# The first four pairs of the feed-forward input: evacuated by ScalarE, multiplied on GpSimd

## The chip, the cores and the metric

One core of one Trainium2 chip runs the whole program. The metric is the device time of one execution in microseconds (us), as the median of several runs. A profile is one further execution, recorded by the hardware profiler. PE is TensorE (its weight loads are PEld), DVE is VectorE, ACT is ScalarE, POOL is GpSimd, SP issues the DMAs of the weights.

## The reference, cut to what matters

A two-layer decoder block on 16 meta tokens and 256 tokens, model width 1024, in float32. Each layer mixes tokens in three branches (retention, a gated linear recurrence, differential attention), and then runs a feed-forward part with a short convolution over time. The change touches only the latter:

```python
def _rms(x):
    xf = x.astype(F32)
    return xf * lax.rsqrt(jnp.mean(xf * xf, axis=-1, keepdims=True) + EPS)

def conv_ffn(hn, w_ffn_in, conv_w, conv_b, w_ffn_out, valid):
    l = hn.shape[1]
    u = jnp.where(valid[None, :, None], hn @ w_ffn_in, 0.0)
    up = jnp.pad(u, ((0, 0), (CONV_W - 1, 0), (0, 0)))
    c = conv_b + sum(conv_w[j] * up[:, j:j + l] for j in range(CONV_W))
    gate, val = jnp.split(c, 2, axis=-1)
    return (jax.nn.silu(gate) * val) @ w_ffn_out

    # per layer
    h = h + mixer(rms_norm(h, norm_mix_g[li]), ...)
    h = h + conv_ffn(rms_norm(h, norm_ffn_g[li]), ...)
```

`w_ffn_in` is 1024 x 5632 (gate and value halves of 2816), `w_ffn_out` 2816 x 1024.

## The kernel before, in words

**Layout.** Activations lie features on partitions, tokens along the free axis: 272 columns in layer 0. In the last layer most projections leave out the first 14 columns, so 258 are computed. Every product of float32 precision is three passes of TensorE over split operands: high part by high part, low part by high part, high part by low part (L900 to L902).

**Weights.** They come as a stream of chunks of eight 128 x 128 tiles in the order of use. For each chunk SP loads `wraw`, ACT rounds it to `whi` (a Copy), and DVE forms the rest `wlo = wraw - whi`. There are 3 buffers of `wraw` and 4 each of `whi` and `wlo`. A chunk feeds 24 matmuls.

**Pairs.** A pair is two output blocks of 128 features that share a PSUM tile `main`, of which there are two. Pair n + 2 writes the tile of pair n, so its first matmul waits until the last reader of pair n is done. A pair of the feed-forward input (name `fi`, 22 in each layer) is 16 weight tiles, thus two chunks and 48 matmuls.

**The norm.** TensorE does not wait for the norm's factor `rstd`. The first four pairs behind a norm multiply by `h` times the gain, and the product gets `rstd` when it leaves PSUM (`evacuate`, which here is a DVE tensor_tensor from `main` into `two_a`). Meanwhile POOL forms `y = h * rstd` in eight instructions, ACT and DVE split each `y` into `xh` and `xl`, and from the fifth pair on the operands are these folded ones (`norm.folded`); then nothing is left to multiply.

**Behind a pair** comes the convolution: ACT writes `two_b` (bias and newest tap, one instruction for each half), DVE adds the two older taps (four SCALAR_TENSOR_TENSOR), ACT applies Silu, DVE multiplies the halves, ACT and DVE split the result into `ghi` and `glo`. For the first four pairs these read `two_a` in SBUF, from the fifth on they read `main` in PSUM. There are two buffers each of `two_a` and `two_b`.

**Order.** No engine's order is written by hand. `_Plan` records all operations with a cost, and `order()` (L448) lists them by a simulated time: on each engine the ready operation with the smallest key goes next. `_Engine.call` (L568) holds the costs. So a changed cost or another operation moves instructions on all engines, and what was once listed is issued in exactly that order, engine by engine, with semaphores between.

**Names with numbers.** The plan numbers its tiles. In layer 0 `main_900`, `main_911`, `main_920` and `main_929` are the first four pairs of the feed-forward input (with `two_a_909`, `_918`, `_927`, `_936` and `two_b_910`, `_919`, `_928`, `_937`), `main_940`, `main_950` and `main_958` the fifth to seventh (`two_b_949`, `two_b_957`, `two_b_965`). In layer 1 the first four are `main_1962`, `_1973`, `_1982`, `_1991` (`two_a_1971`, `_1980`, `_1989`, `_1998`), and the fifth to eighth `main_2002`, `_2012`, `_2020`, `_2028` (`two_b_2011`, `_2019`, `_2027`, `_2035`).

## Time and profile before

| | |
|---|---|
| median of 3 runs (lowest to highest) | 1308.76 us (1308.33 to 1309.17) |
| profiled execution, its own time | 1309.57 us |
| its span, first to last instruction | 1307.8 us |
| granted TensorE clock | 0.999 |
| PE busy | 1295.4 us (99%) |
| DVE busy | 959.0 us (73%) |
| ACT busy | 801.6 us (61%) |
| POOL busy | 169.8 us (13%) |

How to read it: an engine that is busy for 99% of the span sets the time unless its neighbours make it wait, so what matters is where the few microseconds lie in which PE stands still, and who released it. The busy shares of the other engines are averages over stages: in one stage DVE can have no idle time though its share over the whole span is 73%. In the rows of the timeline the columns are start, duration, engine, line, operation, output and inputs, count of merged instructions and, in brackets, idle time before them with the releaser. Instructions of one engine overlap a little (the next one starts before the last one's end is recorded), so the time that one costs its engine is the distance from its start to the next one's.

### The profile page before, as it was taken

To read this page: it belongs to the slowest core of one execution; us is meant where nothing else is said; L and a number is where in the kernel's file an instruction comes from. 1 tells how busy PE (TensorE), PEld (TensorE's weight loads), DVE (VectorE), ACT (ScalarE), POOL (GpSimd) and SP (SyncE) were. 2 spreads that over 40 slices of the span, in tenths; PEclk is the share of its full clock that TensorE was granted. 3 is DMA by queue.
4 is the path that set the end of the run, shared out by engine and by line. 5 is a ranking of instruction groups with operands and counts; after the bars stand their busy time and mean duration, and the time that the engine had idled before them with its cause. 6 is when DMAs were issued, how large, how long until landed. Compare 5 with 4: busy or idle time off the path is not lost.

```text
span 1307.8 us, 28691 instructions
## 1 busy us (share of the span) xinstructions
PE 1295.4 (99%) x11774; PEld 1266.6 (97%) x11774; DVE 959.0 (73%) x1589; ACT 801.6 (61%) x1332; POOL 169.8 (13%) x204
## 2 busy tenths in 40 slices
PE   9999999999999999999999999999999999999998
PEld 8999999999999999999999999999999999999986
DVE  7675787697576789886575757876986867888853
ACT  6747454746676577666456574547565775767643
POOL 5001101312222020000030011012131210200000
PEclk9999999999999999999999999999999999999999
DMA  7644543443544545555555445444445446466553
GB/s 268 202 143 160 168 160 134 146 146 129 193 131 162 179 160 176 182 175 181 177 177 186 162 152 177 150 144 146 156 147 176 142 165 202 144 199 205 200 188 112
DMA packets 60755, 219.06 MB, mean 168 GB/s; under 512 B 6864, under 2 KB 6992, under 8 KB 60624
## 3 DMA queue, kind: packets, MB, share of 16 engines
q1 hardware_dynamic: 60336, 216.71, 49.0%
q8 instruction: 92, 1.51, 0.5%
q10 hardware_dynamic: 288, 0.52, 0.1%
q14 instruction: 39, 0.32, 0.1%
HBM read 216.16 MB, written 1.05 MB: 166 GB/s over the span
## 4 chain that ended last, share of the span: by engine, by line
PE 92%; DVE 5%; ACT 1%; DMA 1%; issue 1%; SPq 0%; POOL 0%; DVEq 0%; ACTq 0%
PE main L900 27%; PE main L902 26%; PE main L901 26%; PE fo L1403 2%; PE fo L1404 2%; PE fo L1405 2%; DVE wlo L592 1%; PE lev L1084 1%; DVE two_b L592 1%; PE ds L1268 1%; PE ro L592 1%; PE ho L592 1%; PE vt L592 1%; DVE two_a L592 1%; PE do L592 1%
## 5 line engine op out<-in xcount | busy, mean ns | idle before, releaser
L900 PE MATMUL main<-xh,whi 128*128 128x272 f32 (+1 forms) x2368 | 689.7, 291 | 0.4 <-ACT whi L592 0.4
L901 PE MATMUL main<-xl,whi 128*128 128x272 f32 (+1 forms) x2368 | 672.9, 284 | 2.0 <-DVE xl L592 2.0
L902 PE MATMUL main<-xh,wlo 128*128 128x272 f32 (+1 forms) x2368 | 673.5, 284 | 1.2 <-DVE wlo L592 1.0
L592 DVE TENSOR_TENSOR wlo<-wraw,whi 128x1024 fp32r<-128x1024 f32 (+1 forms) x411 | 503.4, 1230 | 186.9 <-ACT whi L592 185.9
L592 ACT ACTIVATE whi<-wraw 128x1024 fp32r<-128x1024 f32 (+1 forms) x411 | 427.0, 1042 | 227.7 <-PE main L901 153.4
L901 PEld LDWEIGHTS main<-xl,whi 128*128 128x128 f32 x2368 | 446.1, 188 | 3.0 <-DVE xl L592 2.4
L902 PEld LDWEIGHTS main<-xh,wlo 128*128 128x128 f32 x2368 | 445.8, 188 | 2.8 <-DVE wlo L592 2.7
L900 PEld LDWEIGHTS main<-xh,whi 128*128 128x128 f32 x2368 | 446.2, 188 | 2.1 <-ACT whi L592 0.6
L592 POOL PARTITION_ALL_REDUCE hr<-hsq x36 | 72.0, 2016 | 120.9 <-ACT hsq L592 120.9
L592 DVE SCALAR_TENSOR_TENSOR two_b<-main,small,two_b 128x256 f32<-128x256 f32 (+2 forms) x144 | 65.3, 487 | 26.8 <-ACT two_b L592 25.1
L592 POOL TENSOR_TENSOR y<-h,rstd 128x272 f32<-128x272 f32 x32 | 34.6, 1113 | 317.1 <-ACT rstd L592 317.1
L592 ACT ACTIVATE two_b<-main,small 128x272 f32<-128x272 f32 (+1 forms) x72 | 37.2, 566 | 24.6 <-PE main L902 24.6
L900 PE MATMUL main<-ghi,whi 128*128 128x272 f32 x176 | 51.0, 290 | 0.0
L901 PE MATMUL main<-glo,whi 128*128 128x272 f32 x176 | 50.6, 287 | 0.0
L902 PE MATMUL main<-ghi,wlo 128*128 128x272 f32 x176 | 50.3, 286 | 0.0
L592 POOL COPY tails<-vsrc 128x32 f32<-128x32 f32 x32 | 11.8, 383 | 224.6 <-ACT vsrc L592 224.6
L900 PE MATMUL main<-b0hi,whi 128*128 128x272 f32 (+1 forms) x128 | 38.2, 298 | 0.0
L900 PE MATMUL main<-b1hi,whi 128*128 128x272 f32 (+1 forms) x128 | 37.8, 295 | 0.0
L592 ACT ACTIVATE vsrc<-main 128x544 f32<-128x544 f32 x24 | 15.0, 626 | 35.2 <-PE main L902 35.1
L900 PE MATMUL main<-yhi,whi 128*128 128x272 f32 (+1 forms) x128 | 36.4, 284 | 0.0
L901 PE MATMUL main<-b0lo,whi 128*128 128x272 f32 (+1 forms) x128 | 36.4, 284 | 0.0
L902 PE MATMUL main<-yhi,wlo 128*128 128x272 f32 (+1 forms) x128 | 36.4, 284 | 0.0
(236 smaller groups left out, 1942.3 us busy)
## 6 DMA issues: line engine op xcount, KB each, us to landing
wraw<-in_w SPq DMA_DIRECT2D x402, 512.0 KB, 3.3
h<-in_h SPq DMA_DIRECT2D x4, 272.0 KB, 5.9
dec<-in_dec SPq DMA_DIRECT2D x2, 544.0 KB, 4.9
wraw<-in_w SPq DMA_DIRECT2D x4, 256.0 KB, 5.6
const<-in_const SPq DMA_DIRECT2D x1, 937.0 KB, 6.5
gain<-in_gl SPq DMA_DIRECT2D x1, 512.0 KB, 5.1
out<-y ACTq DMA_DIRECT2D x2, 256.0 KB, 3.0
out<-y SPq DMA_DIRECT2D x2, 256.0 KB, 2.7
```

Source lines behind the costliest of these rows:

```text
L592: self.plan.add(self.name, lambda: f(*args, **kw), cost, outs, ins, args[2] if method == "activation" else None)
L900: nc.tensor.matmul(o, wh, hi, start=first, stop=False)
L901: nc.tensor.matmul(o, wh, lo, start=False, stop=False)
L902: nc.tensor.matmul(o, wl, hi, start=False, stop=last)
L1084: nc.tensor.matmul(o, keys, x, start=True, stop=True)
L1268: nc.tensor.matmul(ss[m][:, at : at + nk], q[half, hd, q0 : q0 + P], k[half, hd, :nk], start=True, stop=True)
L1403: nc.tensor.matmul(o, gh, wh, start=False, stop=False)
L1404: nc.tensor.matmul(o, gl, wh, start=False, stop=False)
L1405: nc.tensor.matmul(o, gh, wl, start=False, stop=end)
```

## The change

`evacuate` gets a flag `aside`, and the feed-forward input passes it. For the first four pairs of that stage, in both layers, the DVE tensor_tensor from PSUM becomes an ACT Copy from `main` to `two_a`, and a POOL tensor_tensor that multiplies `two_a` by `rstd` in place (its key is 2.0 later). That is eight instructions less on DVE, eight more on ACT, eight more on POOL. The plan's costs of POOL change too: a tensor_tensor of n columns goes from 0.04 + 2.45e-3 n to 0.25 + 3.2e-3 n, and a tensor_copy from the same to 0.33 + 0.85e-3 n; the other POOL costs stay.

```diff
             if self.name == "act":
                 cost += 0.093 * (len(aps) - 2) - (0.043 if ins[0].tensor.name in self.plan.psum else 0.0)
-            elif self.name == "pool" and method != "memset":
-                cost += 1.6e-3 * n
+            elif self.name == "pool" and method == "tensor_tensor":
+                cost = 0.25 + 3.2e-3 * n
+            elif self.name == "pool" and method == "tensor_copy":
+                cost = 0.33 + 0.85e-3 * n
...
-    def evacuate(out, ps):
+    def evacuate(out, ps, aside=False):
         factor = pair(rstd[:, T - ps.shape[2] :])
         if norm.folded:
             act.activation(out, ps, AF.Copy)
-        elif norm.adds is pool and norm.pairs == 1:
+        elif aside or norm.adds is pool and norm.pairs == 1:
 
             act.activation(out, ps, AF.Copy)
             plan.key += 2.0
...
-                    evacuate(u, ps)
+                    evacuate(u, ps, True)
```

The branch with ACT and POOL is not new: the very first pair of the program already takes it (`hq`).

The change moves instructions on four of five engines, since the plan is made anew; SP's order stays. Three places matter below. A line of the changed file from the cost rule on has a number higher by two (L594 for L592).

The first place is POOL in layer 0, behind the norm of the feed-forward input. Before, with the copies of the attention's outputs (`da`) ahead of it and the next norm's products behind it:

```order
L592 COPY da_688<-tw_738 128x4x16 x2
L592 ISA
L592 TENSOR_TENSOR y_938<-h_78,rstd_93 128x272 x4
L592 TENSOR_TENSOR y_939<-h_78,rstd_93 128x272 x4
L592 TENSOR_TENSOR y_1202<-h_78,rstd_93 128x272 x4
```

Now:

```order
L594 TENSOR_TENSOR y_938<-h_78,rstd_93 128x272
L594 TENSOR_TENSOR two_a_909<-two_a_909,rstd_93 128x544
L594 TENSOR_TENSOR y_938<-h_78,rstd_93 128x272 x3
L594 TENSOR_TENSOR y_939<-h_78,rstd_93 128x272 x3
L594 TENSOR_TENSOR two_a_918<-two_a_918,rstd_93 128x544
L594 TENSOR_TENSOR y_939<-h_78,rstd_93 128x272
L594 TENSOR_TENSOR two_a_927<-two_a_927,rstd_93 128x544
L594 TENSOR_TENSOR two_a_936<-two_a_936,rstd_93 128x544
```

Four products of 544 columns stand between and behind the eight `y`. In layer 1 the first product (`two_a_1971`) stands ahead of all `y`, the other three behind them.

The second place is DVE in layer 0, around the older taps of the fifth pair (`two_b_949`), the last readers of `main_940`, on which the seventh pair waits. Before:

```order
L592 TENSOR_TENSOR wlo_953<-wraw_951,whi_952 128x1024
L592 SCALAR_TENSOR_TENSOR two_b_937<-two_a_936,small_76,two_b_937 128x271 x2
L592 SCALAR_TENSOR_TENSOR two_b_937<-two_a_936,small_76,two_b_937 128x270 x2
L592 TENSOR_TENSOR wlo_956<-wraw_954,whi_955 128x1024
L592 TENSOR_TENSOR two_b_937<-two_b_937 128x272
L592 SCALAR_TENSOR_TENSOR two_b_949<-main_940,small_76,two_b_949 128x271 x2
L592 SCALAR_TENSOR_TENSOR two_b_949<-main_940,small_76,two_b_949 128x270 x2
L592 TENSOR_TENSOR glo_908<-two_b_937,ghi_907 128x272
L592 TENSOR_TENSOR wlo_961<-wraw_959,whi_960 128x1024
L592 TENSOR_TENSOR two_b_949<-two_b_949 128x272
L592 TENSOR_TENSOR wlo_964<-wraw_962,whi_963 128x1024
```

Now:

```order
L594 TENSOR_TENSOR wlo_956<-wraw_954,whi_955 128x1024
L594 TENSOR_TENSOR two_b_928<-two_b_928 128x272
L594 TENSOR_TENSOR wlo_961<-wraw_959,whi_960 128x1024
L594 TENSOR_TENSOR glo_908<-two_b_928,ghi_907 128x272
L594 SCALAR_TENSOR_TENSOR two_b_937<-two_a_936,small_76,two_b_937 128x271 x2
L594 SCALAR_TENSOR_TENSOR two_b_937<-two_a_936,small_76,two_b_937 128x270 x2
L594 TENSOR_TENSOR wlo_964<-wraw_962,whi_963 128x1024
L594 TENSOR_TENSOR two_b_937<-two_b_937 128x272
L594 SCALAR_TENSOR_TENSOR two_b_949<-main_940,small_76,two_b_949 128x271 x2
L594 SCALAR_TENSOR_TENSOR two_b_949<-main_940,small_76,two_b_949 128x270 x2
L594 TENSOR_TENSOR glo_908<-two_b_937,ghi_907 128x272
```

The weights' rests `wlo_961` and `wlo_964`, both of the seventh pair, stood behind the fifth pair's taps and now stand ahead of them.

The third place is DVE in layer 1, around the older taps of the sixth pair (`two_b_2019`), the last readers of `main_2012`, on which the eighth pair waits. Before:

```order
L592 TENSOR_TENSOR wlo_2026<-wraw_2024,whi_2025 128x1024
L592 TENSOR_TENSOR wlo_2031<-wraw_2029,whi_2030 128x1024
L592 TENSOR_TENSOR glo_2010<-two_b_2011,ghi_2009 128x256
L592 SCALAR_TENSOR_TENSOR two_b_2019<-main_2012,small_76,two_b_2019 128x256 x4
L592 TENSOR_TENSOR wlo_2034<-wraw_2032,whi_2033 128x1024
```

Now:

```order
L594 SCALAR_TENSOR_TENSOR two_b_1999<-two_a_1998,small_76,two_b_1999 128x256 x4
L594 TENSOR_TENSOR two_b_2011<-two_b_2011 128x256
L594 TENSOR_TENSOR wlo_2031<-wraw_2029,whi_2030 128x1024
L594 TENSOR_TENSOR two_b_1999<-two_b_1999 128x256
L594 TENSOR_TENSOR wlo_2034<-wraw_2032,whi_2033 128x1024
L594 TENSOR_TENSOR glo_1970<-two_b_1999,ghi_1969 128x256
L594 TENSOR_TENSOR glo_2010<-two_b_2011,ghi_2009 128x256
L594 TENSOR_TENSOR wlo_2039<-wraw_2037,whi_2038 128x1024
L594 SCALAR_TENSOR_TENSOR two_b_2019<-main_2012,small_76,two_b_2019 128x256 x4
```

Here `wlo_2034` and `wlo_2039` have moved ahead of the sixth pair's taps. Elsewhere, at the start of the program, the two weight chunks of the sixth pair (`wlo_153`, `wlo_156`) and the cast of the masks now stand ahead of the last `xl` piece of the first norm, and PE takes 15 matmuls of the sixth pair ahead of the fifth pair's last six; in layer 1 the softmax steps of the differential attention change places with one another.

## The prediction

> **What bounds the kernel now.** I read the page's first part first, then who PE waited for, then the stretches where those waits lie, then the rows of DVE and POOL there.

> ```profile
> span 1307.8 us, 28691 instructions
> PE 1295.4 (99%) x11774; PEld 1266.6 (97%) x11774; DVE 959.0 (73%) x1589; ACT 801.6 (61%) x1332; POOL 169.8 (13%) x204
> PE main L901 <- DVE xl L592: 2.0, 2, 1.7
> PE main L902 <- DVE wlo L592: 1.0, 4, 0.3
> 490.00:500.00 10.00, 9.64 (x78) 9.41 (x76) 10.00 (x20) 7.60 (x14) 0.00 (x0) 1.00 0.31 108
> 500.00:510.00 10.00, 9.62 (x76) 9.20 (x75) 9.93 (x20) 6.97 (x13) 0.00 (x0) 1.00 0.51 165
> 1130.00:1140.00 10.00, 9.78 (x84) 9.58 (x82) 9.93 (x20) 8.32 (x17) 1.47 (x1) 1.00 0.32 106
> 1140.00:1150.00 10.00, 8.44 (x70) 8.24 (x70) 10.00 (x20) 6.62 (x12) 0.00 (x0) 1.00 0.49 158
> ```

> PE is busy for 99%, so the whole kernel has some 12 us to gain. The columns of the stretches are length, PE, PEld, DVE, ACT, POOL, clock, DMA share and GB/s: around 500 us (layer 0) and 1140 us (layer 1), where the first pairs of the feed-forward input run, PE has holes while DVE has no idle time at all. There DVE is the bound, though its share of the span is 73%. The two largest holes are one late `xl` each:

> ```profile
> 496.19 0.28 PE L900 MATMUL main<-xh,whi 128*128 128x272 f32 x1
> 496.83 0.40 PE L901 MATMUL main<-xl,whi 128*128 128x272 f32 x1 [0.36 <-DVE xl L592]
> 1139.51 0.28 PE L900 MATMUL main<-xh,whi 128*128 128x258 f32 x1
> 1141.44 0.39 PE L901 MATMUL main<-xl,whi 128*128 128x258 f32 x1 [1.66 <-DVE xl L592]
> ```

> Matmuls start 0.12 us apart otherwise, so these cost 0.52 and 1.81 us; the smaller ones on `wlo` behind them some 0.7. About 3.0 us is all that the change could win here. Everything else turns on what DVE loses or gains in these two places, and DVE works beside POOL there:

> ```profile
> 473.31 1.22 DVE L592 TENSOR_TENSOR wlo<-wraw,whi 128x1024 fp32r<-128x1024 f32 x1
> 476.27 0.72 DVE L592 TENSOR_TENSOR two_a<-main,rstd 128x544 f32<-128x544 f32 x1 [1.74 <-ACT rstd L592]
> 476.33 8.47 POOL L592 TENSOR_TENSOR y<-h,rstd 128x272 f32<-128x272 f32 x8 [64.49 <-ACT rstd L592]
> 477.23 1.70 DVE L592 TENSOR_TENSOR wlo<-wraw,whi 128x1024 fp32r<-128x1024 f32 x1 [0.23 <-ACT whi L592]
> 479.60 1.77 DVE L592 TENSOR_TENSOR wlo<-wraw,whi 128x1024 fp32r<-128x1024 f32 x1 [0.67 <-ACT whi L592]
> 481.29 3.80 DVE L592 SCALAR_TENSOR_TENSOR two_b<-two_a,small,two_b 128x271 f32<-128x271 f32 x4
> 485.02 0.71 DVE L592 TENSOR_TENSOR two_a<-main,rstd 128x544 f32<-128x544 f32 x1
> 485.65 0.48 DVE L592 SCALAR_TENSOR_TENSOR xl<-y,small,xh 128x272 fp32r<-128x272 f32 x1
> 493.50 1.73 DVE L592 SCALAR_TENSOR_TENSOR two_b<-two_a,small,two_b 128x271 f32<-128x271 f32 x4
> ```

> While POOL forms `y` (476.3 to 484.8) a `wlo` takes 1.70 and 1.77 us instead of 1.22, and four taps 3.80 instead of 1.73: DVE loses 0.48 + 0.55 + 2.07 = 3.1 us. The evacuation at 476.27, whose product comes from PSUM, takes 0.72 beside POOL and 0.71 alone: it loses nothing. So two engines with operands in SBUF take turns, and an operand in PSUM escapes that. The change removes exactly the DVE work that escapes and gives POOL four longer products of the other kind. How one of these behaves stands at the start of the program:

> ```profile
> 13.98 1.41 POOL L592 TENSOR_TENSOR sum<-sum,two_c 128x544 f32<-128x544 f32 x1 [2.31 <-ACT two_c L592]
> 14.10 2.00 DVE L592 SCALAR_TENSOR_TENSOR xl<-h,small,xh 128x272 fp32r<-128x272 f32 x2
> 29.62 2.39 POOL L592 TENSOR_TENSOR hq<-hq,rstd 128x544 f32<-128x544 f32 x1
> ```

> POOL has the turn at 13.98 and needs 1.41 us; two `xl` behind it take 2.00 instead of 0.83 (0.42 each), so DVE loses 1.2. At 29.62 DVE has the turn and POOL's product lasts 2.39. [...]

> **The change, part by part.** Since PE's matmul work stays, what counts is when DVE passes the point on which PE waits. The new order of DVE decides which point: PSUM has two `main` tiles, and the seventh pair of layer 0 cannot start before the fifth pair's older taps are done, nor the eighth of layer 1 before the sixth's. I sum DVE's time to the end of these taps, each as the distance from start to start.

> ```profile
> 503.53 1.71 DVE L592 SCALAR_TENSOR_TENSOR two_b<-main,small,two_b 128x271 f32<-128x271 f32 x4
> 505.51 1.21 DVE L592 TENSOR_TENSOR wlo<-wraw,whi 128x1024 fp32r<-128x1024 f32 x1
> 506.32 0.29 PE L900 MATMUL main<-xh,whi 128*128 128x272 f32 x1
> 506.65 0.43 DVE L592 TENSOR_TENSOR two_b<-two_b 128x272 f32<-128x272 f32 x1
> ```

> Layer 0. The taps end at 503.53 + 1.71 = 505.24, and the seventh pair starts at 506.32, 1.1 later and without a wait for them.
> (a) Two more `wlo` stand ahead of them (`wlo_961`, `wlo_964`), 1.14 each (505.51 to 506.65): +2.3.
> (b) Four evacuations go, 0.63 each (485.02 to 485.65): -2.5.
> (c) Four POOL products. The first falls half into a time when DVE has nothing to do, +0.7; the others meet a busy DVE, 1.3 each: +4.6 in all. The bounds are 0 (all in gaps) and 4 x 1.41 = 5.6; I am near the top, because DVE is 100% busy in the stretch.
> (d) The eight `y` (0.76 alone, 8 x 0.75 = 6.0) cost DVE 3.1 before, because it evacuated or waited meanwhile. Now seven of them meet SBUF work: 5.2, so +2.1; bounds 0 and 2.9.
> (e) ACT's copy (0.63, as `vsrc` below) now stands between `rstd` and the next `whi`, so DVE's gap behind 474.5 grows by 0.6. The gap is idle time: from it (c) and (d) have had their share already.

> ```profile
> L592 ACT ACTIVATE vsrc<-main 128x544 f32<-128x544 f32 x24 | 15.0, 626 | 35.2 <-PE main L902 35.1
> ```

> Sum: +7.1, the taps end near 512.3 instead of 505.2, and the seventh pair starts 6.0 late. From that go 0.2 for a small wait that stood behind it: **+5.8 us**. The holes of 0.5 at 496 and 500 lie within this, since PE cannot be late twice. Behind it DVE needs less than PE for each pair, so nothing adds up.

> Layer 1, with the eighth pair at 1156.03:

> ```profile
> 1120.52 1.23 DVE L592 TENSOR_TENSOR wlo<-wraw,whi 128x1024 fp32r<-128x1024 f32 x1 [1.34 <-ACT whi L592]
> 1122.78 0.69 DVE L592 TENSOR_TENSOR two_a<-main,rstd 128x516 f32<-128x516 f32 x1 [1.04 <-ACT rstd L592]
> 1122.84 8.63 POOL L592 TENSOR_TENSOR y<-h,rstd 128x272 f32<-128x272 f32 x8 [63.37 <-ACT rstd L592]
> 1123.81 1.62 DVE L592 TENSOR_TENSOR wlo<-wraw,whi 128x1024 fp32r<-128x1024 f32 x1 [0.33 <-ACT whi L592]
> 1125.35 3.75 DVE L592 SCALAR_TENSOR_TENSOR two_b<-two_a,small,two_b 128x256 f32<-128x256 f32 x4
> 1130.76 1.42 DVE L592 SCALAR_TENSOR_TENSOR xl<-y,small,xh 128x272 fp32r<-128x272 f32 x2
> 1153.65 1.65 DVE L592 SCALAR_TENSOR_TENSOR two_b<-main,small,two_b 128x256 f32<-128x256 f32 x4
> 1156.03 0.28 PE L900 MATMUL main<-xh,whi 128*128 128x258 f32 x1
> ```

> The sixth pair's taps end at 1155.3. (a) `wlo_2034` and `wlo_2039` come ahead: +2.3. (b) -2.4. (c) The first product falls mostly into DVE's gap, +0.4, then three of 1.33: +4.4. (d) All eight `y` now stand behind it and meet a busy DVE: 5.9 against 3.0 before (0.4 at 1123.81, 2.1 at 1125.35, 0.5 at 1130.76): +2.9. (e) The `whi` for the `wlo` of 1120.52 moves behind `rstd`, so DVE stands from 1119.2 to about 1123.4, 4.2 us, instead of 1.3 + 1.0 + 0.3: +1.5. Sum +8.7: the taps end near 1164.0, the eighth pair starts **8.0 us** late, with the 1.81 of 1141 inside.

> The start. The last `xl` piece of the first norm ended at 34.47, where the next `wlo` starts. Now `rstd` comes 1.1 later, because DVE's sum of squares waits behind one `wlo` more, and three `wlo` (3.4), an evacuation (0.6) and the masks' cast (0.3) stand ahead of the piece: 39.9. PE wanted it at 32.55 + 7 x 0.74 = 37.7, and 15 matmuls put ahead move that to 39.5: **+0.4**; bounds 0 and 2 (if those 15 wait as well, for `wlo_153`).

> ```profile
> 32.55 0.28 PE L900 MATMUL main<-xh,whi 128*128 128x272 f32 x1
> 34.47 1.23 DVE L592 TENSOR_TENSOR wlo<-wraw,whi 128x1024 fp32r<-128x1024 f32 x1
> ```

> ACT's eight copies (5.0 us in all) cost nothing by themselves: ACT is busy 6.6 to 8.3 of 10 us there, and what they delay stands in (e). POOL's own time too is free, being 13% busy. DMA queues: SP's order is the same. The attention of layer 1, whose softmax steps change places, I put at 0: PE waited there for at most 0.3 us at a time (row below), and the plan spreads this work to end 12 us (`MARGIN`) ahead of its use. It can give -1 or +3.

> ```profile
> PE do L592 <- DVE tw L592: 0.3, 1, 0.3
> ```

> Sum: 0.4 + 5.8 + 8.0 = 14.2 on the profiled execution's 1309.57 (its span is 1307.8, the rest lies around it): 1323.8. The median of the runs is 0.8 below that execution: 1323.0. I forecast **1322**, since each holding point can be passed a little sooner when a product of POOL falls into a wait of DVE.

> **The rivals.** (1) Half of the turns fall into gaps, or are shared. Then (c) and (d) are 3.4 and 3.7: layer 0 gets to 509.0 and loses 2.5, layer 1 to 1160.3 and loses 4.3; with 0.4 that is +7.2, 1316. For it: POOL could start its products while DVE waits for ACT. Against it: DVE's 9.93 to 10.00 of 10.

> (2) POOL takes nothing from DVE, and only the order counts: (a) + (b) + (e) are +0.4 and +1.4. Layer 0's taps end at 505.6, before 506.32, and its holes go (-1); layer 1 loses 0.7, the start 0.4. In all +0.1: 1309. Against it stands the 2.00 at 14.10.

> (3) The other side, faster: DVE keeps the 2.5 us that each layer saves, and its `xl` and `wlo` are in time. Then the 3.0 us of holes go: 1305.8. It decides where the four products cost DVE less than 2.5 us per layer and no `wlo` moved ahead of taps makes a pair wait. For it: the new order has most `xl` ahead of the third pair's taps. Against it: both rows of POOL's products above. [...]

> (4) Worse: the attention or the start wait too, or a held `two_a` makes ACT late with `main_1991`: over 1327.

> **How the numbers follow.** Forecast (1317 to 1327) 0.60; rival 1 (1311.4 to 1317) 0.22; rival 2 0.06; rival 3 0.04; rival 4 0.08. The range 1313.5 to 1327 takes in the forecast, and rival 1 down to where two thirds of (c) and (d) are hidden. A measurement of this kernel tells 0.2% (2.6 us) from no change: faster (below 1306.1) 0.04, the same 0.06, slower 0.90.

> **What would show it.** Right: the group of POOL `two_a<-two_a,rstd` has a mean well over 1.4 us, near 2; four taps from `two_a` take about 3 us rather than 1.73 wherever a product runs; PE waits for DVE `two_b` near 506 to 512 and 1156 to 1164, and each wait is several us; PE's busy time stays 1295. Term (c) is wrong if the taps beside those products take 1.73 for four. Term (a) is wrong if the seventh and eighth pair start without a wait. The forecast falls if PE's waits in the two places stay near 3 us, or if the loss lies in the attention.

## The result, and the profile after

| | before | after |
|---|---|---|
| median (lowest to highest) | 1308.97 us (1308.33 to 1309.44) | 1322.21 us (1321.23 to 1323.50) |
| ratio, 95% interval | | 1.0101 (1.0089 to 1.0114) |
| profiled execution, its span | 1309.57, 1307.8 us | 1321.78, 1320.0 us |
| granted clock | 0.999 | 0.995 |

The change costs 13.2 us; the kernel takes 1322.2 us, and 1322 was forecast. (The two profiled executions lie only 12.2 us apart: the one before is 0.6 us above its kernel's median, the one after 0.4 below.) The busy times from the page of the changed kernel, and below them who PE waited for (engine, line, releaser: us in all, times, longest):

```profile
PE 1300.3 (99%) x11774; PEld 1271.9 (96%) x11774; DVE 960.6 (73%) x1581; ACT 805.9 (61%) x1340; POOL 189.8 (14%) x212
```

```profile
PE main L902 <- ACT two_b L594: 3.7, 1, 3.7
PE main L902 <- DVE two_b L594: 3.0, 2, 2.6
PE main L902 <- ACT two_a L594: 2.8, 1, 2.8
PE main L904 <- DVE wlo L594: 1.1, 2, 0.9
```

The three waits at the top are new, and two of them are where the prediction looked for them. But PE is also busy for 1300.3 us instead of 1295.4, with the same 11774 matmuls. The timeline of PE in the changed kernel, around the seventh pair of layer 0, shows both:

```profile
505.47 0.28 PE L904 MATMUL main<-xh,wlo 128*128 128x272 f32 x1
509.45 0.57 PE L902 MATMUL main<-xh,whi 128*128 128x272 f32 x1 [3.69 <-ACT two_b L594]
509.81 0.43 PE L903 MATMUL main<-xl,whi 128*128 128x272 f32 x1
510.04 0.43 PE L904 MATMUL main<-xh,wlo 128*128 128x272 f32 x1
...
517.92 0.29 PE L904 MATMUL main<-xh,wlo 128*128 128x272 f32 x1
```

After the pause the matmuls start 0.23 us apart, not 0.12, and the pair needs 517.92 - 509.45 = 8.47 us; before it ran from 506.32 to 512.44. The stretches of the changed kernel say why; behind the busy times stand the granted clock, the DMA share and GB/s:

```profile
508.00:508.30 0.30, 0.00 (x0) 0.00 (x0) 0.30 (x2) 0.30 (x2) 0.00 (x0) 1.00 0.00 0
508.30:509.40 1.10, 0.00 (x0) 0.00 (x0) 1.10 (x4) 1.10 (x2) 0.00 (x0) 0.50 0.82 276
509.40:515.10 5.70, 5.65 (x25) 5.68 (x26) 4.86 (x9) 1.56 (x5) 0.00 (x0) 0.50 0.60 203
515.10:515.40 0.30, 0.30 (x4) 0.30 (x4) 0.00 (x0) 0.30 (x1) 0.00 (x0) 0.96 0.72 287
```

While PE stands, its clock falls to half at 508.3 and comes back at 515.1: it is the granted clock of TensorE, 0.50 of the full one in these rows. What kept the pair waiting is seen in the timelines of POOL and DVE (the profile puts the wait down to ACT, whose `two_b` of the fifth pair was done at 505.7; the reader that came last is DVE's tap):

```profile
476.38 1.35 POOL L594 TENSOR_TENSOR two_a<-two_a,rstd 128x544 f32<-128x544 f32 x1
484.84 1.57 POOL L594 TENSOR_TENSOR two_a<-two_a,rstd 128x544 f32<-128x544 f32 x1
489.54 1.61 POOL L594 TENSOR_TENSOR two_a<-two_a,rstd 128x544 f32<-128x544 f32 x1 [1.41 <-issue]
496.96 2.72 POOL L594 TENSOR_TENSOR two_a<-two_a,rstd 128x544 f32<-128x544 f32 x1 [5.81 <-ACT two_a L594]
```

```profile
477.04 1.77 DVE L594 TENSOR_TENSOR wlo<-wraw,whi 128x1024 fp32r<-128x1024 f32 x1 [3.20 <-ACT whi L594]
485.10 2.39 DVE L594 TENSOR_TENSOR wlo<-wraw,whi 128x1024 fp32r<-128x1024 f32 x1
489.84 2.44 DVE L594 SCALAR_TENSOR_TENSOR xl<-y,small,xh 128x272 fp32r<-128x272 f32 x3
495.63 1.32 DVE L594 SCALAR_TENSOR_TENSOR xl<-y,small,xh 128x272 fp32r<-128x272 f32 x3
497.22 1.22 DVE L594 TENSOR_TENSOR wlo<-wraw,whi 128x1024 fp32r<-128x1024 f32 x1
498.36 1.62 DVE L594 SCALAR_TENSOR_TENSOR two_b<-two_a,small,two_b 128x271 f32<-128x271 f32 x1
504.47 1.72 DVE L594 SCALAR_TENSOR_TENSOR two_b<-two_a,small,two_b 128x271 f32<-128x271 f32 x4
507.60 1.70 DVE L594 SCALAR_TENSOR_TENSOR two_b<-main,small,two_b 128x271 f32<-128x271 f32 x4
```

Each of the three products that meet a busy DVE delays one DVE instruction: a `wlo` by 2.39 - 1.21 = 1.18, the first of three `xl` by 2.44 - 1.32 = 1.12, one tap by 1.62 - 0.49 = 1.13 us. The first product starts in DVE's gap; only its second half meets the `wlo` of 477.04 and delays it by 1.77 - 1.21 = 0.56 us. The fifth pair's taps end at 507.60 + 1.70 = 509.30, and PE goes on at 509.45.

Layer 1, the same engines:

```profile
1127.34 1.30 POOL L594 TENSOR_TENSOR two_a<-two_a,rstd 128x516 f32<-128x516 f32 x1 [61.43 <-issue]
1138.33 3.75 POOL L594 TENSOR_TENSOR two_a<-two_a,rstd 128x516 f32<-128x516 f32 x2
1151.09 5.63 POOL L594 TENSOR_TENSOR two_a<-two_a,rstd 128x516 f32<-128x516 f32 x1 [9.01 <-ACT two_a L594]
```

```profile
1128.19 1.54 DVE L594 TENSOR_TENSOR wlo<-wraw,whi 128x1024 fp32r<-128x1024 f32 x1 [4.22 <-ACT whi L594]
1138.59 2.33 DVE L594 TENSOR_TENSOR wlo<-wraw,whi 128x1024 fp32r<-128x1024 f32 x1
1140.84 1.52 DVE L594 TENSOR_TENSOR glo<-two_b,ghi 128x256 fp32r<-128x256 f32 x1
...
1155.48 1.65 DVE L594 SCALAR_TENSOR_TENSOR two_b<-main,small,two_b 128x256 f32<-128x256 f32 x4
...
1163.98 2.44 DVE L594 SCALAR_TENSOR_TENSOR two_b<-main,small,two_b 128x256 f32<-128x256 f32 x6
```

```profile
1151.01 0.39 PE L902 MATMUL main<-xh,whi 128*128 128x258 f32 x1 [2.84 <-ACT two_a L594]
...
1165.78 0.36 PE L902 MATMUL main<-xh,whi 128*128 128x258 f32 x1 [2.64 <-DVE two_b L594]
```

Two products cost DVE 1.1 us each (2.33 - 1.21, 1.52 - 0.42), the first 0.32 (1.54 - 1.22), the last nothing: there it is GpSimd that takes 5.63 us. PE waits twice: before the sixth pair for ACT's copy of the fourth (it needs a `two_a`, and there are two), and before the eighth pair for the sixth's taps, the first four of the six at 1163.98. The eighth pair then loses 1.7 us to half clock (7.2 us for 5.5).

### The profile page after: what moved, and what is told of

It reads as the page before. It is cut to its first block, busy times and chain, and to the rows that moved or that the text cites. A ratio compares the mean times of both kernels' runs of the same rounds, so it can differ in the third digit from the quotient of the medians.

```text
span 1320.0 us, 28706 instructions
## 1 busy us (share of the span) xinstructions
PE 1300.3 (99%) x11774; PEld 1271.9 (96%) x11774; DVE 960.6 (73%) x1581; ACT 805.9 (61%) x1340; POOL 189.8 (14%) x212
## 4 chain that ended last, share of the span: by engine, by line
PE 91%; DVE 6%; issue 1%; DMA 1%; ACT 0%; SPq 0%; DVEq 0%; ACTq 0%
PE main L902 27%; PE main L903 26%; PE main L904 26%; DVE wlo L594 2%; DVE two_b L594 2%; PE fo L1407 2%; PE fo L1406 2%; PE fo L1405 2%; PE lev L1086 1%; PE ds L1270 1%; PE ro L594 1%; PE ho L594 1%; DMA wraw<-in_w 1%; PE vt L594 1%; PE do L594 1%
## 5 line engine op out<-in xcount | busy, mean ns | idle before, releaser
L902 PE MATMUL main<-xh,whi 128*128 128x272 f32 (+1 forms) x2368 | 692.7, 293 | 9.6 <-ACT two_b L594 3.7
L594 DVE TENSOR_TENSOR wlo<-wraw,whi 128x1024 fp32r<-128x1024 f32 (+1 forms) x411 | 505.9, 1236 | 197.4 <-ACT whi L594 195.8
L594 ACT ACTIVATE whi<-wraw 128x1024 fp32r<-128x1024 f32 (+1 forms) x411 | 427.3, 1043 | 229.3 <-PE main L903 154.1
L902 PEld LDWEIGHTS main<-xh,whi 128*128 128x128 f32 x2368 | 447.9, 189 | 11.7 <-ACT two_b L594 3.9
L594 POOL PARTITION_ALL_REDUCE hr<-hsq x36 | 73.8, 2069 | 124.0 <-ACT hsq L594 124.0
L594 DVE SCALAR_TENSOR_TENSOR two_b<-main,small,two_b 128x256 f32<-128x256 f32 (+2 forms) x144 | 66.2, 488 | 32.8 <-ACT two_b L594 30.7
L594 POOL TENSOR_TENSOR y<-h,rstd 128x272 f32<-128x272 f32 x32 | 37.8, 1212 | 246.1 <-ACT rstd L594 246.1
L594 ACT ACTIVATE two_b<-main,small 128x272 f32<-128x272 f32 (+1 forms) x72 | 37.1, 568 | 30.5 <-PE main L904 29.9
L902 PE MATMUL main<-ghi,whi 128*128 128x272 f32 x176 | 51.0, 290 | 0.0
L594 POOL COPY tails<-vsrc 128x32 f32<-128x32 f32 x32 | 11.7, 380 | 222.6 <-ACT vsrc L594 222.5
L902 PE MATMUL main<-b0hi,whi 128*128 128x272 f32 (+1 forms) x128 | 38.3, 299 | 0.0
L902 PE MATMUL main<-b1hi,whi 128*128 128x272 f32 (+1 forms) x128 | 38.0, 297 | 0.0
L902 PE MATMUL main<-yhi,whi 128*128 128x272 f32 (+1 forms) x128 | 36.4, 284 | 0.0
L904 PE MATMUL main<-b0hi,wlo 128*128 128x272 f32 (+1 forms) x128 | 36.4, 284 | 0.0
```

Of the source, the lines that this page charges most:

```text
L594: self.plan.add(self.name, lambda: f(*args, **kw), cost, outs, ins, args[2] if method == "activation" else None)
L902: nc.tensor.matmul(o, wh, hi, start=first, stop=False)
L904: nc.tensor.matmul(o, wl, hi, start=False, stop=last)
```

## The experiments

All against the kernel before in the same runs; median, and ratio with its interval:

| | us | ratio |
|---|---|---|
| costs_only | 1308.35 | 0.9996 (0.9987 to 1.0006) |
| aside_only | 1316.45 | 1.0058 (1.0043 to 1.0073) |
| pool_short | 1310.11 | 1.0008 (0.9998 to 1.0017) |
| pool_write | 1311.64 | 1.0021 (1.0011 to 1.0030) |
| fill | 1319.01 | 1.0076 (1.0061 to 1.0091) |
| taps_first | 1315.74 | 1.0054 (1.0040 to 1.0067) |
| aside_l0 | 1313.85 | 1.0039 (1.0026 to 1.0053) |
| aside_first | 1310.13 | 1.0010 (1.0001 to 1.0018) |
| defer5 | 1307.52 | 0.9991 (0.9982 to 1.0000) |
| defer5_costs | 1306.88 | 0.9986 (0.9977 to 0.9995) |

### The two edits apart

costs_only: the changed kernel with `evacuate(u, ps)` as before.

> The new plan costs of GpSimd without the new evacuation: eight DVE evacuations as before. Against the kernel before only the start of the program moves (sum of squares, first evacuation, masks, the sixth pair's chunks). The prediction's term for the start says +0.4 (bounds 0 to 2): 1309.4. The trace of the changed kernel, whose tiles stand 0.4 earlier behind the start, says -0.4: 1308.6. If the costs were what makes the changed kernel late, it would come near 1322.

aside_only: the changed kernel with the old cost rule (`cost += 1.6e-3 * n`).

> The new evacuation with the old plan costs. If the two parts do not touch each other, this is the changed kernel without its start: 1322.2 + 0.4 = 1322.6 by the trace of the changed kernel, 1321.8 by the prediction's +0.4, and both pauses before the seventh pair of layer 0 and the eighth of layer 1 are there with 3 to 4 us. If the late pairs come from the plan made with the new costs, it stays near 1309.

The costs alone make no difference that can be told, -0.6 us; it points the other way than the start's +0.4. The new evacuation alone costs 7.5, not 13: both numbers of the expectation missed. The two edits do not add up (-0.6 + 7.5 against 13.2). In aside_only DVE is late as well, but its taps stand earlier in the order, and PE waits for `xl` of the fifth pair, in layer 0 without loss of clock (1.00 from 495 to 515) and in layer 1 with it (half clock from 1143.8 to 1150.6). PE of aside_only:

```profile
PE main L901 <- DVE xl L592: 6.2, 3, 2.5
```

```profile
1145.50 0.58 PE L901 MATMUL main<-xl,whi 128*128 128x258 f32 x1 [2.48 <-DVE xl L592]
```

So for this evacuation the order made with the new costs is the worse one, by 5.8 us: it puts the weights' rests `wlo` ahead of the taps.

### The turns

pool_short keeps every engine's order and shortens what the eight products touch:

```diff
-            pool.tensor_tensor(out=out, in0=out, in1=factor, op=MUL)
+            pool.tensor_tensor(out=out, in0=out, in1=factor, op=MUL, cut=16 if aside else T)
```

(`cut` slices the operands to so many columns of each half, so the factor is left out for the other columns; the plan still sees the full cost.)

> The changed kernel in its own order, but each of the eight GpSimd products of two_a multiplies only the first 16 tokens of its two halves (32 columns instead of 544 or 516), so the factor is left out for the other tokens. Theory of turns: the products' turns are what makes DVE late; three of them met a busy DVE in each layer, some 1.1 to 1.4 each, so the fifth pair's taps in layer 0 end near 505.5 to 506.5 instead of 509.3 and the seventh pair starts nearly without a wait, the eighth of layer 1 too; with the clock kept as well 1310 to 1313. Rival 2 (the order alone makes the pairs late): 1321 to 1322, and the taps end near 509 as in the changed kernel. Half of the lateness from turns: about 1316.

1310.11. The fifth pair's taps of layer 0 end at 503.38 + 1.71 = 505.09 and the seventh pair starts nearly in time; the eighth of layer 1 still waits. Taps and PE of pool_short:

```profile
503.38 1.71 DVE L594 SCALAR_TENSOR_TENSOR two_b<-main,small,two_b 128x271 f32<-128x271 f32 x4
```

```profile
505.24 0.36 PE L902 MATMUL main<-xh,whi 128*128 128x272 f32 x1 [0.91 <-DVE two_b L594]
...
1155.77 0.36 PE L902 MATMUL main<-xh,whi 128*128 128x258 f32 x1 [2.28 <-DVE two_b L594]
```

The length of the products carries 12.1 of the 13.2 us, so rival 2 (the order alone) is out. A shorter product also ends sooner and keeps GpSimd less busy. pool_write tells that apart:

```diff
+                    for _ in range(4):
+                        nc.gpsimd.memset(scratch, 0.0)
                     nc.gpsimd.tensor_tensor(out=o, in0=o, in1=x, op=MUL)
```

> As pool_short (products of 32 columns, the factor left out for the other tokens), but ahead of each short product GpSimd writes zeros to an unused SBUF tile for about 1.2 us (four memsets of 256 columns at 0.31), so that it is busy as long as in the changed kernel, without reading SBUF. Turns of two readers: DVE's instructions beside the memsets keep their 0.49 and 1.21 us, and it comes out like pool_short, 1310 to 1311. Rival: GpSimd's being busy, or the product's later end, is what makes DVE late: near 1320.

POOL and DVE of pool_write:

```profile
487.88 1.42 POOL L926 MEMSET scratch<- 128x256 f32 x4
489.27 1.46 POOL L927 TENSOR_TENSOR two_a<-two_a,rstd 128x32 f32<-128x32 f32 x1
```

```profile
488.16 1.32 DVE L594 SCALAR_TENSOR_TENSOR xl<-y,small,xh 128x272 fp32r<-128x272 f32 x3
489.40 1.21 DVE L594 TENSOR_TENSOR wlo<-wraw,whi 128x1024 fp32r<-128x1024 f32 x1
```

Beside 1.42 us of writing, three `xl` need 1.32 us, as they do alone (495.63 above). The product of 32 columns behind it needs 1.46 where pool_short has 0.45 to 0.81 in that layer, and it ends 0.12 us behind a `wlo` that took its 1.21 as alone (489.40): here it is GpSimd that waited. 1311.64 is 1.5 us more than pool_short (where these lie is open), and 10.6 less than the changed kernel. GpSimd's being busy with writes is not the cause; how long it reads SBUF is.

### The clock

fill: behind the sixth pair of layer 0 and the seventh of layer 1 PE gets work that nobody reads.

```diff
+FILL = {(False, "fi", 5): 30, (True, "fi", 6): 22}
...
                 nc.tensor.matmul(o, wl, hi, start=False, stop=last)
+                for _ in range(n):
+                    nc.tensor.matmul(fb, x[:, :P], x[:, t0:], start=True, stop=True)
```

> The changed kernel in its own order with idle work on PE: 30 matmuls of 272 columns behind the sixth pair of layer 0 (30 x 0.1225 = 3.7 us, into the wait of 3.9) and 22 behind the seventh pair of layer 1 (2.6 us, into the wait of 2.9), written to a PSUM bank that nobody reads. Theory of the clock: the granted clock falls to half because PE pauses; without the pause the seventh pair takes 6.0 us instead of 8.5 and the eighth 5.5 instead of 7.2, so 2.5 + 1.7 less: 1318. Rival: the clock falls for another reason (the DMA load or DVE's burst there): the two stretches at half clock stay, 1322 or a little more.

PE of fill, and its stretches:

```profile
506.47 3.92 PE L910 MATMUL fill<-xh 128*128 128x272 f32 x30
510.34 0.36 PE L906 MATMUL main<-xh,whi 128*128 128x272 f32 x1
```

```profile
510.00:515.00 5.00, 5.00 (x42) 4.86 (x41) 5.00 (x10) 3.34 (x7) 0.00 (x0) 1.00 0.57 179
1150.00:1155.00 5.00, 5.00 (x33) 5.00 (x33) 5.00 (x10) 1.86 (x5) 4.96 (x1) 0.72 0.61 189
1165.00:1170.00 5.00, 5.00 (x45) 5.00 (x44) 3.81 (x8) 2.21 (x4) 0.00 (x0) 1.00 0.46 169
```

Both pairs keep the full clock now (42 and 45 matmuls in 5 us), the seventh needs 5.88 us instead of 8.47, with DVE as full as it was: the clock is 1.00 where it was 0.50 and 0.71, so the pause took it. The gain is 3.2 us and not 4.2; in the profiled execution the sixth pair of layer 1, whose wait was not filled, loses the clock (0.72) though it had not in the changed kernel.

### The order

taps_first: one `wlo` in layer 0 and two in layer 1 go back behind the taps; nothing else moves.

```diff
+SWAP = ((("two_b_436", "main_433"), ("wlo149",)), (("two_b_894", "main_893"), ("wlo353", "wlo354")))
...
+                order.remove(o)
+                order.insert(order.index(last) + 1, o)
```

(these are the plan's own names of `two_b_949`, `main_940`, `wlo_964`, and of `two_b_2019`, `main_2012`, `wlo_2034`, `wlo_2039`)

> The changed kernel, but on DVE one weight rest of layer 0 (wlo_964) and two of layer 1 (wlo_2034, wlo_2039) are issued behind the older taps on which the seventh and the eighth pair wait, as they stood before the change. This undoes half of the prediction's term (a) in layer 0 (1.14 us) and all of it in layer 1 (2.28 us). Theory (a): the fifth pair's taps end at 508.2 instead of 509.30, the sixth's near 1163 instead of 1165.6, the two waits shrink from 3.9 and 2.9 to 2.8 and 0.6, and the half clock in layer 1 (1.7 us) goes: 1317. Rival: what the rests gain the taps they cost the next chunk, so PE waits for wlo instead, and it stays at 1321 to 1322.

1315.74, 6.5 us less. Who PE waited for in taps_first:

```profile
PE main L909 <- DVE two_b L601: 4.0, 2, 2.8
PE main L909 <- ACT two_a L601: 2.8, 1, 2.8
PE main L911 <- DVE wlo L601: 1.3, 3, 0.9
```

The two waits fall from 3.7 and 2.6 to 2.8 and 1.2, the waits for `wlo` hardly grow, and the eighth pair keeps its clock (1.00 from 1165 to 1170). Three instructions of 1.2 us in another place are worth half of the loss while the turns are there; with the turns nearly taken away (pool_short) all of the new order costs 1.2 us, which the interval there does not tell from nothing.

### Where it may be put

> The new evacuation in layer 0 only, new plan costs; layer 0's order of DVE is that of the changed kernel, layer 1's that of the kernel with the new costs alone. If the layers add up: layer 0's part of the changed kernel is its shift behind the seventh pair, +5.5, of which 2.5 is the half clock: 1308.4 + 6.2 (from the 0.7 that it was ahead) = 1314.6, with the wait of 3.9 and the half clock before and in the seventh pair. Rival: layer 1's part is only a consequence of layer 0's lateness, so that without layer 1's change it still comes near 1318 or more.

(`evacuate(u, ps, li == 0)`) 1313.85: +5.5 over costs_only, where layer 0's part had been put at 6.2. The waits of aside_l0 hold the 3.7 us of the seventh pair, and in layer 1 the `xl` of the kernel before:

```profile
PE main L902 <- DVE two_b L594: 3.7, 1, 3.7
PE main L903 <- DVE xl L594: 1.7, 1, 1.7
```

Layer 1's part is thus its own, not a consequence.

> The new evacuation for the first pair of each layer only, whose product falls into the 3 to 4 us in which DVE waits for the norm's factor; pairs two to four leave by DVE as before; new plan costs. Theory of turns: the first product costs DVE next to nothing and saves 0.63 us of it, but the eight y come 1.35 us later and meet more of its work (+0.7): no change, 1308 to 1310, and no pause of several us. Rival: any GpSimd product here makes the fifth or sixth pair late: 1312 to 1315.

(`evacuate(u, ps, j == 0)`) 1310.13, just above the 1308 to 1310 that were expected: no pause of several us, but 1.2 us slower than before all the same; the longest waits are 1.2 for an `xl` and 1.1 for a `wlo`. So even with only the product that falls mostly into DVE's gap it does not pay.

### A version that beats both

DVE's time in these stretches is the bound, and taking evacuations off it with GpSimd's help made the kernel slower in these runs (by 1.2 us in aside_first, 13.2 in the changed kernel). One thing left is to move the due time of what DVE does there. `DEFER` is the number of pairs behind a norm that still multiply unfolded operands:

```diff
-DEFER = 4
+DEFER = 5
```

> The kernel before, with the operands folded from the sixth pair of each norm on instead of the fifth (DEFER 5 for 4): DVE's evacuation with the factor stays, whose product from PSUM loses nothing beside GpSimd, there is one more of it behind each norm (0.63 us), and the last xl, for which the fifth pair waits 0.5 us in layer 0 and 1.8 in layer 1, is due one pair (5.8 us) later. If the bound is DVE's lateness at those xl, the 3.0 us of holes shrink and the added 0.63 per norm lies in the slack behind: 1306 to 1308. Rival: the evacuation more makes the taps late that the next pairs wait for, as the products did in the changed kernel: 1309 to 1312.

> The same (DEFER 5, all evacuations by DVE) with the changed kernel's plan costs of GpSimd. Alone these costs made 1308.35 of 1308.95, no difference that this measurement tells. If the two add up: as defer5, less 0 to 0.6: 1305.5 to 1308. Rival: the plan with the longer y puts the xl later again and the holes come back: 1308 to 1311.

1307.52 and 1306.88. Only the second, with the new costs, is faster than before by more than its interval: 1.9 us, 0.14%. Its waits, where before there were 2.0 us for `xl`:

```profile
PE main L903 <- DVE xl L594: 0.9, 2, 0.6
```

## Why the prediction was right, and where its sizes were off

**Direction and places: right.** PE's new waits stand before the seventh pair of layer 0 and the eighth of layer 1, for the taps of the pairs two before them, as worked out from PSUM's two `main` tiles.

**(c) The products' turns: right in kind, too large.** They were put at 1.3 us each, +4.6 and +4.4. Measured: 1.1 for each of five that met a busy DVE, 0.56 and 0.32 for the first of each layer (put at 0.7 and 0.4), and nothing for the last of layer 1: 4.0 and 2.5. That last one, put at 1.33, is the largest single miss: it did not get the turn. It lasted 5.63 us beside DVE instructions that took no longer than alone. It was done 1.24 us after DVE turned at 1155.48 to taps that read PSUM, about as long as a product takes alone (1.30 at 1127.34). So GpSimd may also be the one that waits, here behind six DVE instructions in a row and elsewhere behind one (2.72 us at 496.96), as DVE is at 485.10 (2.39 us for a `wlo`); what decides that, no run shows. The mean of the products was expected near 2 us and is 1.8 in layer 0 and 2.7 in layer 1:

```profile
L594 POOL TENSOR_TENSOR two_a<-two_a,rstd 128x516 f32<-128x516 f32 x4 | 10.7, 2679 | 70.4 <-issue 61.4 <-ACT two_a L594 9.0
L594 POOL TENSOR_TENSOR two_a<-two_a,rstd 128x544 f32<-128x544 f32 x4 | 7.3, 1814 | 7.2 <-ACT two_a L594 5.8 <-issue 1.4
```

**(d) The eight `y`: too large.** Put at +2.1 and +2.9. Summed over DVE's instructions in the stretch, what they took beyond their time alone beside a `y` is 3.4 instead of 3.1 us in layer 0 and 4.1 instead of 3.0 in layer 1: +0.3 and +1.1. Much of it DVE already lost before.

**(a), (b), (e): as priced.** DVE's gap in layer 1 was put at 4.2 us and is 4.22. (a) looked like 2.3 us; its worth depends on the rest, as taps_first (6.5 us) and pool_short (1.2) show. That DVE is late by about the sum of the terms, as measured, holds (next paragraph); that PE loses no more than its wait does not, since the clock comes on top.

**The sums.** Layer 0's taps came 4.1 us late and not 7.1; the measured terms give 2.3 - 2.5 + 4.0 + 0.3 + 0.6 = 4.7, less 0.7 by which the program was ahead. In layer 1 they give 2.3 - 2.4 + 2.5 + 1.1 + 1.5 = 5.0, and the taps lost 5.5. The seventh pair, 0.7 ahead, started 3.1 late (3.8 in all, for 5.8 forecast); the eighth of layer 1 went from 4.8 to 9.75 late (5.0, for 8.0).

**What was missing: the clock.** PE's busy time was to stay at 1295. The pauses took the clock, and this cost another 2.4 us in layer 0 and 1.7 in layer 1, so that the layers came to 6.2 and 6.7 where 5.8 and 8.0 were forecast. With the start at -0.7 instead of +0.4 the three make 12.2, the difference of the spans (the attention of layer 1, put at 0, gave back 0.7, and the end of the program took as much). That the total is so near the forecast is in good part luck: two misses of opposite sign met, (c) and (d) too large by 6.1 in both layers together, the clock's 4.1 not there.

**Rival 1** had half of the turns hidden, (c) and (d) at 3.4 and 3.7. Measured they are 4.3 in layer 0 and 3.6 in layer 1: on the turns it was nearer than the forecast. That half was the author's estimate, and no run shows a shared turn: a product of 1.35 us took 1.1 from a DVE instruction that it met, and nothing where GpSimd was the one that waited. Its 1316 lacks the same 4.1 us of clock, and with them it would stand at 1320.

**The held `two_a`,** named in rival 4, happened: the 2.84 us before the sixth pair of layer 1. It probably did not add up with the wait behind it, since DVE, which had no idle time from there to the sixth pair's taps but 0.26 us, is as late either way. A third `two_a` buffer was not tried.

**The plan.** The prediction looked at its new costs only through the order that they make. They are not GpSimd's times alone: for a product of 544 columns they give 1.99 us where the old rule gave 1.37 and 476.38 above took 1.35. They are nearer to the mean beside a busy DVE (2.25 us over the eight products). So the plan lets GpSimd lose time to the turns and charges DVE nothing; by these costs it placed three `wlo` where they cost most (taps_first). Whether a plan that charges DVE for the turns would do better was not tried.

## What to carry to other kernels

An engine's share of the whole span says little about what may be moved to it: GpSimd was 13% busy, and five of its eight products each took 1.1 us from a DVE that was full in just that stretch, more than the 0.63 us evacuation that had gone. Before moving work, look at whether both engines read SBUF in the same microseconds. And price a wait of TensorE of 2.6 us or more at up to 1.65 times its length, as the clock may fall behind it: here waits of 3.69 and 2.64 us cost 2.4 and 1.7 us more. Where an engine is full for some 30 us, look at the order of its single instructions too: moving three of 1.2 us gained 6.5.

## What the runs showed of the hardware that was not expected

A pause of 2.28 us (pool_short before the eighth pair) and one of 2.64 (the changed kernel) took the clock, while one of 2.84 (the changed kernel, 1148.2 to 1151.0) did not, and the same wait of 2.8 did in fill (0.72 from 1150 to 1155). So the length alone does not decide. In the changed kernel a border lies at 1150.0, five pieces ahead of the fall at 1167.07, and divides the pause of 2.84 into 1.8 and 1.0 us. In the pieces that end where the clock fell, PE stood for 2.5 and 2.1 us (the changed kernel), 2.2 (pool_short) and 2.0 in two pauses (aside_only); how the pauses of the other runs lie to the borders is not shown. In the kernel before and the changed one, the longest that PE stood in a piece at full clock without a fall behind it is 1.66 and 1.83 us; between 1.83 and 2.0 us nothing was measured. A second piece at half clock followed where PE also stood for 1.15 us (the changed kernel, 508.30 to 509.45) and 1.7 us (aside_only) in the first, and none where PE was busy throughout (3.30 of 3.30 us in the changed kernel behind 1167.1 and in pool_short behind 1157.0). This is a reading of these pauses; no run placed a pause to test it.
